# Four quadrants for v's and the inverse's products, new side durations in the planner, two loads on SP's queue, and overwritten products ahead of two transposes, in a two-layer RWKV, pooling and attention trunk

## The chip, the core and the metric

The kernel runs on one core of a Trainium2 chip. A time is the device time of one execution in microseconds; the kernel before is given by the median of three runs. The engines are named as the profile names them: PE (TensorE), ACT (ScalarE), DVE (VectorE), POOL (GpSimd) and SP (SyncE, which only issues DMAs here).

## What is computed

Input x is 1 x 1024 x 1024 in float32. Each of two layers makes one wide projection of x and feeds three branches with it, whose gated sum goes through an output projection and a normalization:

```python
for l in range(DEPTH):
    h = jnp.einsum('bsd,dn->bsn', x, w_in[l]) + b_in[l]
    (u_a, z_a, p_b, z_b, q_c, k_c, v_c, z_c, g_a, g_b, g_c) = _split(h, SPLIT_SIZES)
    o_a = rwkv7_branch(u_a, z_a, ...)
    o_b = pool_branch(p_b, z_b, ...)
    o_c = attention_branch(q_c, k_c, v_c, z_c, cos, sin)
    merged = (sigmoid(g_a) * (o_a @ proj_a[l]) + sigmoid(g_b) * (o_b @ proj_b[l])
              + sigmoid(g_c) * (o_c @ proj_c[l]))
    x = normalize(DEEPNORM_ALPHA * x + merged @ w_out[l]) * ln_g[l] + ln_b[l]
```

The RWKV branch is the long one. For 16 heads of 64, forwards and backwards over 1024 positions, it carries a 64x64 state: `sa = state @ (-kk)`, then `state = state * w + sa b^T + v k^T` and `y = state @ r`. The kernel does it in chunks of 64 positions, which needs the inverse of a triangular matrix in each chunk, and a sequential step over the chunks.

## The kernel before

**Dense products.** Every weight matrix is used in float32 by three products: the weight is split into a high part `wh` (a cast on ACT, L551) and a low part `wl` (a subtraction, L552, on POOL in the RWKV stage and the merge, on POOL or DVE elsewhere), the activations likewise into `xh` and `xl` (or `obh`/`obl`, `och`/`ocl`, `mh`/`ml`). A dense step is three products of 128x512 over one block of 128 rows: L583 (high, high), L584 (low, high) and L585 (high, low). `Dense` makes these steps; a piece of weight is 128x512 values, loaded by SP at L540.

**Stages.** A layer runs `rwkv` (848 dense steps with the recurrence between them), `attention`, `pool`, `proj_bc` (projections of the two branches behind pooling and attention, gated) and `merge` (projection proj_a, the gated sum, then w_out and the normalization, token block by token block). In layer 0 they stand at about 60 to 1222, 1222 to 1600, to 1758, 1758 to 1859 and 1859 to 2065 us; layer 1 follows in the same way.

**What sets the order.** Each engine works through its own queue in order. The order is made when the program is built: pieces of work (`Th`) have a list of steps with an engine and a cost in ns each ("P" PE, "A" ACT, "D" DVE, "G" POOL, "S" SP), needs and gives, and buffers in rings ("m" is a ring of two PSUM buffers of 2 KB per partition). `Sched.run` simulates the engines with these costs and takes what can start soonest, with dense steps as filler. A `side` cost is what a dense step books on other engines (the split of the weight piece). So a changed cost moves instructions on all engines, though it is no instruction itself.

**The recurrence.** For each of 8 pairs of heads (`j`) and 4 quarters (`q`) of the sequence, both directions are prepared together: scores, the inverse by products in f16 (L1054), `nkt` (32 transposes by products with the identity, L1008, two PSUM buffers, two copies) and `av` (16 products of a score block with v, L1022, one PSUM buffer, one copy at L1025); the trace shows each float32 product of this form as two. Then four steps each follow: `A` (products of the state, L1143 and L1146, into the two PSUM tiles `sqp`, `pu` and `py`; then DVE adds u0, L1150), `W` (ACT scales the state, L1154), `B` (four products, L1161, then two ACT copies into `uv`, L1165) and `Cc` (L1175, L1180, then DVE updates the state, L1185). There are 64 `av` and 256 steps in the two layers. `HS[0]` and `HS[1]` are partitions 0 to 63 and 64 to 127: the rows of an operand choose the row half of the array, the partitions of the result the column half, so a 64x64 product takes one quadrant of the array. In `nkt` the products of a group take all four quadrants; in `av` and `B` they take two.

```python
1022  nc.tensor.matmul(ps[HS[h], d, i], lhsT=sc[HS[1 - h], d, c, h, 0:64], rhs=uv[HS[1 - h], n, h, :], ...)
1161  nc.tensor.matmul(pu[HS[h], 128 + 64 * s:192 + 64 * s], lhsT=J["sc", Q][HS[h], d, c, 0, 0:64], rhs=J["u0"][HS[h], d, :], ...)
```

The quarter's end is normalized and transposed (`f5`, L1246, four transposes from `ysq`, which POOL writes at L1241). At the start of each pair, `psk` (L781) and `psr` (L823, from `nx`, which ACT writes at L796) make norms and the rotated copies.

**The other places.** In `attention`, `t1` makes the scores (L1447) from `rawq` and `rawk`, to which DVE applies the rotary embedding (`rope`, L1387 to L1394). In `proj_bc`, ACT writes the high and POOL the low part of `oz`, the result of the RWKV branch, from 32 loads `ozt` (L1772 issues, L1776 casts, L1778 subtracts); the products of `obh` and `och` are gated by DVE (`m`, L1741; `t`, L1752) and added by POOL (L1754). `y` at L1692 is DVE's last product on the pooling branch. In `merge`, `wor` (L1819) loads 16 blocks of w_out, the products of a token block follow (L1842 to L1844), DVE reads the gate `g` at L1810, and `back` (L1883) transposes the normalized block `s`, which POOL finishes at L1873, for the next layer.

Of the kernel before, what the change touches and what calls it, by code (L numbers as in the profile page):

```python
# [10 lines left out]
F32 = mybir.dt.float32  # L11
# [371 lines left out]
def trunk(ctx: ExitStack, tc: tile.TileContext, a: dict, out, dbg=None):  # L383
# [124 lines left out]
    class Dense:  # L508
# [56 lines left out]
        def make(self, src, nk, rhs, evac, halves=(0, 1), needs=(), gives=(), ev=(("A", 570.0),), key=None, ering=(), first=False):  # L565
# [31 lines left out]
            for x in range(len(ids) * len(halves)):  # L597
                for pi, h in [(x % len(ids), halves[x // len(ids)]) if first else (x // len(halves), halves[x % len(halves)])]:
                    for kk in range(min(KP, nk - KP * pi)):
                        last = KP * pi + kk == nk - 1  # L600
                        out_.append(Th(mm(pi, kk, h), [("P", 640.0)],
                                       side=(("A", 307.0), ("G" if self.lo is nc.gpsimd else "D", 620.0 if self.lo is nc.gpsimd else 335.0)) if kk == 0 and h == halves[0] else (),
# [25 lines left out]
    def rwkv(l):  # L628
        P = pc["P"]
        w_in = a["w_in"][l]  # L630
        with ExitStack() as es:
# [136 lines left out]
            def pair_kk(j):  # L768
# [76 lines left out]
                o.append(Th(f5, [("G", 3770.0)]))  # L845
# [151 lines left out]
            def joint(j, q):  # L997
# [16 lines left out]
                def av():  # L1014

                    sc, ps = J["sc", Q], psm.tile([128, 2, 4, 64], F32, tag="m", name="psav")
                    uv = J["uv", j, int(q in (1, 2))]
                    for d in range(2):
                        for i in range(4):
                            c, n, _ = place(d, q, i)  # L1020
                            for h in range(2):
                                nc.tensor.matmul(ps[HS[h], d, i], lhsT=sc[HS[1 - h], d, c, h, 0:64], rhs=uv[HS[1 - h], n, h, :],  # L1022
                                                 start=True, stop=True, skip_group_check=True)
                    yield
                    nc.scalar.copy(sc[:, :, :, 1, 0:64], ps)  # L1025
                return ([Th(nkt, [("P", 930.0), ("A", 500.0), ("A", 500.0)], needs=[("sc", d, Q) for d in range(2)], ring=("m", "m"), gives=[("nkt", Q)])],
                        [Th(av, [("P", 930.0), ("A", 500.0)], needs=[("nt", Q), ("uv" if q in (1, 2) else "uv0", j)], ring=("m",), gives=[("av", Q)])])
# [95 lines left out]
            def seq(j, q):  # L1123
# [4 lines left out]
                def step(i):  # L1128
# [6 lines left out]
                    def A():  # L1135
# [4 lines left out]
                        for d in range(2):  # L1140
                            ar, (c, n, s) = J["ar", d, Q % NB], pl[d]
                            for h in range(2):
                                nc.tensor.matmul(pu[HS[h], 64 * d:64 * d + 64], lhsT=ar[HS[h], c, 0, :], rhs=sbd[d][HS[h]],  # L1143
                                                 start=d == 0, stop=True, skip_group_check=True)
                            for h in range(2):
                                nc.tensor.matmul(py[HS[1 - h], y0 + 64 * s:y0 + 64 * s + 64], lhsT=ar[HS[h], c, 1, :], rhs=sbd[d][HS[h]],  # L1146
                                                 start=d == 0, stop=False, skip_group_check=True)
# [8 lines left out]
                    def B():  # L1156
                        pu, uv = J["p"][1], J["uv", j, io]
                        for d in range(2):
                            c, n, s = pl[d]
                            for h in range(2):  # L1160
                                nc.tensor.matmul(pu[HS[h], 128 + 64 * s:192 + 64 * s], lhsT=J["sc", Q][HS[h], d, c, 0, 0:64], rhs=J["u0"][HS[h], d, :],  # L1161
                                                 start=False, stop=True, skip_group_check=True)
# [804 lines left out]
```

## Time and profile before

| | |
|---|---|
| median of 3 runs | 4117.68 us (4116.34 to 4122.85) |
| profiled execution | 4110.03 us, its span 4107.9 us |
| mean granted PE clock over the span | 0.990 |
| PE busy | 3933.5 us, 96% |
| ACT, DVE, POOL busy | 2224.0, 2344.7, 1653.9 us |
| DMA | 326.41 MB, mean 79 GB/s |

The busy share is a mean over stages with different limits. A row of the timeline gives start and length of an instruction or of a group of like ones; a bracket behind it, as [2.95 <-DVE rawk L1394], says how long the engine had been idle and what ended that. In the table by stretches PEclk is the granted clock as a share of full speed: 0.5 is a stretch wholly at 1.2 GHz, 1.00 one at 2.4. Durations and sums below come from the profiled execution.

### The profile page before, as it was taken

What the parts mean: (1) busy time and instruction counts of PE and PEld (TensorE: products, weight loads), DVE (VectorE), ACT (ScalarE), POOL (GpSimd) and SP (SyncE); (2) the same over time, 40 slices, a digit from 0 to 9 for tenths busy, and PEclk for the clock granted to TensorE, in tenths of its full rate; (3) what the DMA queues carried; (4) which work ended last, traced back from release to release, by engine and by line L of the source; (5) the groups of instructions that cost most, each with busy time, mean ns of one, the idle gap of its engine ahead of it and who ended that gap; (6) DMA issues with size and microseconds to landing.
All of it is one profiled execution on the core that took longest, in us unless ns stands there. A gap on an engine that the chain in (4) does not pass through costs nothing. (4 is left out here: it accounts for less than half of the span.)

```text
span 4107.9 us, 120670 instructions
## 1 busy us (share of the span) xinstructions
PE 3933.5 (96%) x51576; PEld 3060.1 (74%) x51576; DVE 2344.7 (57%) x4233; ACT 2224.0 (54%) x4390; POOL 1653.9 (40%) x2498
## 2 busy tenths in 40 slices
PE   8999999999999999999989999999999999999998
PEld 6677777777777788877767777777777777888777
DVE  3776766665533554545647667766665245454456
ACT  5677787777643442322146777777677434433210
POOL 4343444344433343453233444454434334334532
PEclk9999999999999999999999999999999999999999
DMA  2111111111114442155311111111111244421653
GB/s 90 32 48 43 44 42 45 45 42 44 58 58 119 130 134 91 54 181 192 123 51 30 48 40 44 42 48 40 43 47 54 76 114 133 127 83 55 191 182 116
DMA packets 329192, 326.41 MB, mean 79 GB/s; under 512 B 23536, under 2 KB 264384, under 8 KB 328655
## 3 DMA queue, kind: packets, MB, share of 16 engines
q1 hardware_dynamic: 301551, 233.66, 19.1%
q0 software_dynamic: 27104, 85.04, 5.9%
q8 instruction: 404, 6.62, 0.7%
q14 instruction: 133, 1.09, 0.1%
HBM read 224.86 MB, written 81.99 MB: 75 GB/s over the span
## 5 line engine op out<-in xcount | busy, mean ns | idle before, releaser
L583 PE MATMUL psdn<-xh,wh 128*128 128x512 f32 x3136 | 1331.1, 424 | 9.1 <-ACT wh L551 8.2
L585 PE MATMUL psdn<-xh,wl 128*128 128x512 f32 x3136 | 1240.8, 396 | 9.5 <-POOL wl L552 9.3
L584 PE MATMUL psdn<-xl,wh 128*128 128x512 f32 x3136 | 1236.5, 394 | 0.0
L552 POOL TENSOR_TENSOR wl<-wr,wh 128x512 fp32r<-128x512 f32 (+1 forms) x436 | 599.4, 1375 | 1313.1 <-ACT wh L551 1287.5
L583 PEld LDWEIGHTS psdn<-xh,wh 128*128 128x128 f32 x3136 | 594.5, 190 | 169.0 <-issue 31.0
L585 PEld LDWEIGHTS psdn<-xh,wl 128*128 128x128 f32 x3136 | 593.8, 189 | 151.4 <-POOL wl L552 19.5
L584 PEld LDWEIGHTS psdn<-xl,wh 128*128 128x128 f32 x3136 | 596.2, 190 | 101.0 <-issue 4.8
L551 ACT CAST wh<-wr 128x512 fp32r<-128x512 f32 (+2 forms) x484 | 290.3, 600 | 697.6 <-PE psdn L584 351.1
L1059 ACT CAST U<-pst 64x512 f16<-64x512 f32 x768 | 444.8, 579 | 116.9 <-PE pst L1054 100.1
L1087 DVE TENSOR_TENSOR X<-pst,c 128x512 f16<-128x512 f32 x320 | 219.4, 685 | 198.2 <-PE pst L1054 198.1
L1185 DVE SCALAR_TENSOR_TENSOR sbd<-sqp,wc,sbd 128x64 f32<-128x64 f32 x480 | 113.8, 278 | 216.9 <-PE sqp L1180 156.4
L1165 ACT COPY uv<-sqp 64x128 f32<-64x128 f32 x512 | 131.5, 257 | 85.0 <-PE sqp L1161 76.9
L1054 PEld LDWEIGHTS <-X 64*64 64x64 f16 x6144 | 144.1, 108 | 26.6 <-DVE sc L983 8.4
L1154 ACT ACTIVATE sbd<-sbd,wc 128x64 f32<-128x64 f32 x480 | 140.3, 340 | 43.1 <-PE sqp L1146 30.6
L1071 POOL TENSOR_TENSOR nl<-sc,nh 64x512 f16<-64x512 f32 x128 | 154.7, 1209 | 8.2 <-ACT nh L1068 3.0
L1054 PE MATMUL pst<-U,X 64*64 64x64 f16 x5120 | 153.6, 197 | 2.1 <-ACT U L1059 0.9
L1161 PEld LDWEIGHTS sqp<-u,sc 64*64 64x64 f32 x2048 | 80.1, 133 | 91.4 <-issue 50.2
L978 PE MATMUL pssc<-ar,nk 64*64 64x128 f32 x4096 | 146.4, 274 | 0.4
L1054 PEld LDWEIGHTS <-U 64*64 64x64 f16 x5120 | 113.1, 109 | 44.9 <-issue 14.5
L1054 PE MATMUL pst<-X,U 64*64 64x64 f16 x5120 | 140.3, 194 | 0.3
L1143 PEld LDWEIGHTS sqp<-sbd,ar 64*64 64x64 f32 x2048 | 83.6, 133 | 73.9 <-issue 43.7
L1150 DVE TENSOR_TENSOR u<-sqp,sc 128x128 f32<-128x128 f32 x256 | 73.4, 287 | 113.5 <-PE sqp L1146 61.0
(707 smaller groups left out, 7707.5 us busy)
## 6 DMA issues: line engine op xcount, KB each, us to landing
wr<-in_w_in_dram SPq DMA_DIRECT2D x360, 256.0 KB, 2.9
sga<-gt POOLq DMA_DIRECT2D x96, 256.0 KB, 2.3
g<-sga SPq DMA_DIRECT2D x96, 256.0 KB, 4.4
wr<-in_proj_a_dram SPq DMA_DIRECT2D x64, 256.0 KB, 3.0
sza<-sz POOLq DMA_DIRECT2D x32, 256.0 KB, 3.2
bva<-bv POOLq DMA_DIRECT2D x32, 256.0 KB, 2.5
oa<-o POOLq DMA_DIRECT2D x32, 256.0 KB, 3.0
oat<-oa SPq DMA_DIRECT2D x32, 256.0 KB, 3.6
```

The source lines that it names most:

```text
L551: nc.scalar.copy(hi[:, 0:n, :], r[:, 0:n, :])
L552: self.lo.tensor_tensor(out=lo[:, 0:n, :], in0=r[:, 0:n, :], in1=hi[:, 0:n, :], op=ALU.subtract)
L583: nc.tensor.matmul(ps, lhsT=hi[:, kk, :], rhs=ah, start=(k == 0), stop=False)
L584: nc.tensor.matmul(ps, lhsT=hi[:, kk, :], rhs=al, start=False, stop=False)
L585: nc.tensor.matmul(ps, lhsT=lo[:, kk, :], rhs=ah, start=False, stop=(k == nk - 1))
L978: nc.tensor.matmul(ps[h][HS[h if x == 0 else 1 - h], c, :], lhsT=nk[HS[h], c, x, :], rhs=ar[HS[h], c].rearrange("p a t -> p (a t)"), start ...
L1054: nc.tensor.matmul(ps[HS[1 - h if mir else h], d, c], lhsT=l, rhs=r, start=start and d == 0 and c == 0, stop=stop, skip_group_check=True)
L1059: nc.scalar.copy(dst[HS[h]], ps[HS[1 - h]])
L1071: nc.gpsimd.tensor_tensor(out=nl[HS[h]], in0=sc[HS[h], :, :, h, 0:64], in1=nh[HS[h]], op=ALU.subtract)
L1087: tt(out=x, in0=ps[0], in1=mask(i + 1), op=ALU.mult)
L1154: act(sbd[d], sbd[d], AF.Copy, scale=J["wc", d, Q % NB][:, pl[d][0]:pl[d][0] + 1])
L1165: nc.scalar.copy(uv[HS[h], two, h, :], pu[HS[h], 128:256].rearrange("p (s e) -> p s e", s=2))
```

## The change

1. `av`: products of the two directions alternate, into one PSUM buffer each, and those of direction 1 write the other half of the partitions, so the group takes four quadrants; one copy of 128x512 becomes one of 128x256 and two of 64x256.
2. `B`: the products go by row half to the one or the other `sqp` tile and by direction to the upper or lower partitions, four quadrants; two copies of 64x128 become four of 64x64. In `A`, the products for `py` come ahead of those for `pu`.
3. The planner's costs: the split of a weight piece goes from 307 to 520 ns on ACT, from 620 to 1235 on POOL and from 335 to 602 on DVE, and many others are raised (rope's three DVE steps from 1160 each to 1900, 2070 and 1500).
4. The loads of `ozt` (32) and `wor` (16) are issued by SP in place of POOL.
5. Ahead of the last `f5` of each layer's RWKV stage stand 12 products of 128x512 into the buffer that the transposes then overwrite, and ahead of the first `back` of the last token block of layer 0 stand 20.

Lines move: L1161 is L1164 after, L1165 L1169, L1022 L1023, L1025 L1026 and L1029, L1246 L1252 (its 12 products L1250), L1447 L1453, L1692 L1698, L1772 L1778, L1776 L1782, L1883 L1891 (its 20 products L1889).

```diff
@@ Dense: side cost of a piece
-   side=(("A", 307.0), ("G" if ... else "D", 620.0 if ... else 335.0)) ...
+   side=(("A", 520.0), ("G" if ... else "D", 1235.0 if ... else 602.0)) ...
@@ av
-   sc, ps = J["sc", Q], psm.tile([128, 2, 4, 64], F32, tag="m", name="psav")
+   ps = [psm.tile([128, 4, 64], F32, tag="m", name="psav") for _ in range(2)]
-   for d in range(2):
-       for i in range(4):
+   for i in range(4):
+       for d in range(2):
            for h in range(2):
-               nc.tensor.matmul(ps[HS[h], d, i], lhsT=sc[HS[1 - h], d, c, h, 0:64], ...)
+               nc.tensor.matmul(ps[d][HS[h if d == 0 else 1 - h], i], lhsT=sc[HS[1 - h], d, c, h, 0:64], ...)
-   nc.scalar.copy(sc[:, :, :, 1, 0:64], ps)
+   nc.scalar.copy(sc[:, 0, :, 1, 0:64], ps[0])
+   yield "first"
+   for h in range(2):
+       nc.scalar.copy(sc[HS[h], 1, :, 1, 0:64], ps[1][HS[1 - h]])
@@ step B
-   pu, uv = J["p"][1], J["uv", j, io]
+   p, uv = J["p"][::-1], J["uv", j, io]
-   nc.tensor.matmul(pu[HS[h], 128 + 64 * s:192 + 64 * s], ...)
+   nc.tensor.matmul(p[h][HS[d], 384:448], ...)
-   nc.scalar.copy(uv[HS[h], two, h, :], pu[HS[h], 128:256].rearrange("p (s e) -> p s e", s=2))
+   for d in range(2):
+       nc.scalar.copy(uv[HS[h], pl[d][1], h, :], p[h][HS[d], 384:448])
@@ f5
+   for _ in range(12 if j == NJ - 1 and o == 0 else 0):
+       nc.tensor.matmul(ps.rearrange("p a b -> p (a b)"), lhsT=xh[:, 0, 0:128], rhs=xh[:, 0, 0:512], start=True, stop=True)
@@ rope
-   Th(f1, [("D", 1160.0)]), Th(f2, [("D", 1160.0)]), Th(f3, [("D", 1160.0)], ...)
+   Th(f1, [("D", 1900.0)]), Th(f2, [("D", 2070.0)]), Th(f3, [("D", 1500.0)], ...)
@@ proj_bc, loads of oz
-   nc.gpsimd.dma_start(out=t, in_=oz[k * 128:(k + 1) * 128, hs])
+   nc.sync.dma_start(out=t, in_=oz[k * 128:(k + 1) * 128, hs])
-   load.append(Th(fn, [("G", 1040.0)], lag=LDW, ...))
+   load.append(Th(fn, [("S", 100.0)], lag=LDW, ...))
@@ merge, loads of w_out
-   nc.gpsimd.dma_start(out=t, in_=a["w_out"][l][k * 128:(k + 1) * 128, :])
+   nc.sync.dma_start(out=t, in_=a["w_out"][l][k * 128:(k + 1) * 128, :])
@@ back
+   for _ in range(20 if t == 7 and g == 0 else 0):
+       nc.tensor.matmul(ps.rearrange("p a b -> p (a b)"), lhsT=mh[:, 0, 0:128], rhs=wh[:, 0, 0:512], start=True, stop=True)
```

PE, one step of the recurrence in layer 0: `A`'s products, dense steps, then `B`'s, of before and after (`pu` is `sqp_1641` before and `sqp_1660` after, `py` is `sqp_1640` and `sqp_1659`).

```order
L1143 MATMUL sqp_1641<-sbd0_294,ar_889 64x64 x2
L1146 MATMUL sqp_1640<-sbd0_294,ar_889 64x64 x2
L1143 MATMUL sqp_1641<-sbd1_295,ar_895 64x64 x2
L1146 MATMUL sqp_1640<-sbd1_295,ar_895 64x64 x2
L781 MATMUL psk_1650<-cst_80,sq_1575 128x128 x4
L583 MATMUL psdn_1661<-xh_88,wh_1278 128x512
L584 MATMUL psdn_1661<-xl_89,wh_1278 128x512
L585 MATMUL psdn_1661<-xh_88,wl_1279 128x512
L583 MATMUL psdn_1661<-xh_88,wh_1278 128x512
L584 MATMUL psdn_1661<-xl_89,wh_1278 128x512
L585 MATMUL psdn_1661<-xh_88,wl_1279 128x512
L1161 MATMUL sqp_1641<-u0_1655,sc_949 64x64 x4
```

```order
L1150 MATMUL sqp_1660<-sbd1_295,ar_895 64x64 x2
L583 MATMUL psdn_1634<-xh_88,wh_1236 128x512
L584 MATMUL psdn_1634<-xl_89,wh_1236 128x512
L585 MATMUL psdn_1634<-xh_88,wl_1237 128x512
L583 MATMUL psdn_1634<-xh_88,wh_1236 128x512
L584 MATMUL psdn_1634<-xl_89,wh_1236 128x512
L585 MATMUL psdn_1634<-xh_88,wl_1237 128x512
L1164 MATMUL sqp_1660<-u0_1672,sc_949 64x64
L1164 MATMUL sqp_1659<-u0_1672,sc_949 64x64
L1164 MATMUL sqp_1660<-u0_1672,sc_949 64x64
L1164 MATMUL sqp_1659<-u0_1672,sc_949 64x64
```

`B`'s four products, all into one PSUM tile before, alternate between the two tiles; two dense steps stand ahead of them in both.

PE, the first score products of the attention stage in layer 0 (`pssc`), with the dense products ahead of them (a new number at `psdn` begins a new dense tile), of before and after.

```order
L583 MATMUL psdn_23443<-xh_88,wh_23419 128x512
L584 MATMUL psdn_23443<-xl_89,wh_23419 128x512
L585 MATMUL psdn_23443<-xh_88,wl_23420 128x512
L1447 MATMUL pssc_23485<-rawk_23407,rawq_23327 128x128
L1447 MATMUL pssc_23486<-rawk_23407,rawq_23327 128x128
```

```order
L585 MATMUL psdn_23807<-xh_88,wl_23784 128x512
L583 MATMUL psdn_23855<-xh_88,wh_23820 128x512
L584 MATMUL psdn_23855<-xl_89,wh_23820 128x512
L585 MATMUL psdn_23855<-xh_88,wl_23821 128x512
L583 MATMUL psdn_23855<-xh_88,wh_23820 128x512
L584 MATMUL psdn_23855<-xl_89,wh_23820 128x512
L585 MATMUL psdn_23855<-xh_88,wl_23821 128x512
L1453 MATMUL pssc_23869<-rawk_23770,rawq_23691 128x128
L1453 MATMUL pssc_23870<-rawk_23770,rawq_23691 128x128
```

Before, two steps of the second half's last piece (`psdn_23443`) were still to come behind these products; now that tile is done and two steps of the next are ahead of them: four dense steps later. The first score products of the second, third and fifth tile also move back four steps, those of the fourth and sixth one step.

ACT, the beginning of `proj_bc` in layer 0, of before and after (`y` are the last evacuations of the pooling branch, `wh` the casts of proj_b's and proj_c's pieces, 128x512 and 128x256).

```order
L1689 ACTIVATE y<-psdn,pc 128x512 x2
L551 CAST wh<-wr 128x512
L551 CAST wh<-wr 128x256 x2
L1776 CAST xh<-ozt 128x512 x2
L551 CAST wh<-wr 128x512
L1776 CAST xh<-ozt 128x512
```

```order
L1695 ACTIVATE y<-psdn,pc 128x512 x2
L1782 CAST xh<-ozt 128x512
L551 CAST wh<-wr 128x512
L1782 CAST xh<-ozt 128x512 x2
L551 CAST wh<-wr 128x256
L1782 CAST xh<-ozt 128x512 x3
```

The cast of the first 128x512 piece now stands behind the first cast from `ozt`, which waits for a load that SP issues. On PE, the last `psy` transposes of the RWKV stage stand ten dense steps later than before, and in `merge` SP issues the `wor` loads singly between those of the weights and of the gates.

## Rows read from the trace of the kernel before

**Rows 1.** The page, part 1: busy us, share of the span, instructions.
```profile
PE 3933.5 (96%) x51576; PEld 3060.1 (74%) x51576; DVE 2344.7 (57%) x4233; ACT 2224.0 (54%) x4390; POOL 1653.9 (40%) x2498
```

**Rows 2.** Windows, first RWKV stage: stretch, us, busy by engine, PEclk, DMA share, GB/s.
```profile
130.00:1210.00 1080.00, 1055.24 (x21368) 792.97 (x21365) 691.06 (x1439) 794.59 (x1649) 449.94 (x849) 1.00 0.14 44
200.00:300.00 100.00, 99.39 (x1968) 75.24 (x1964) 73.37 (x142) 80.93 (x165) 49.80 (x99) 1.00 0.14 44
```

**Rows 3.** Timeline, PE: start us, length us, line, operation, count of products.
```profile
427.62 1.16 PE L1008 MATMUL psnt<-cst,nk 64*64 64x64 f32 x64
...
603.35 0.45 PE L1161 MATMUL sqp<-u,sc 64*64 64x64 f32 x8
...
664.45 1.15 PE L1022 MATMUL psav<-uv,sc 64*64 64x64 f32 x32
```

**Rows 4.** Groups by line and form, ACT: busy us, mean ns | idle before.
```profile
L1165 ACT COPY uv<-sqp 64x128 f32<-64x128 f32 x512 | 131.5, 257 | 85.0 <-PE sqp L1161 76.9
...
L758 ACT COPY uv<-psv 64x256 f32<-64x256 f32 x128 | 46.9, 366 | 9.7 <-PE psv L753 7.8
...
L1025 ACT COPY sc<-psav 128x512 f32<-128x512 f32 x64 | 37.4, 584 | 32.2 <-PE psav L1022 16.3 <-POOL nl L1071 8.6 <-PE sqp L1146 4.7
```

**Rows 5.** Timeline, PE, attention of layer 0: [idle before <- what ended it].
```profile
1263.61 2.02 PE L1447 MATMUL pssc<-rawk,rawq 64*128 64x128 f32 x16 [2.95 <-DVE rawk L1394]
...
1406.39 1.46 PE L1447 MATMUL pssc<-rawk,rawq 64*128 64x256 f32 x8 [2.69 <-DVE rawk L1394]
...
1458.23 1.14 PE L1447 MATMUL pssc<-rawk,rawq 64*128 64x256 f32 x8 [0.77 <-DVE rawk L1394]
```

**Rows 6.** Timeline, PE, layer 0: RWKV stage's ends, merge's end.
```profile
67.61 0.66 PE L781 MATMUL psk<-cst,sq 128*128 128x128 f32 x4 [1.28 <-ACT lw L915]
...
80.24 1.12 PE L823 MATMUL psr<-cst,nx 128*128 128x128 f32 x4 [5.89 <-ACT nx L796]
...
1214.83 0.39 PE L583 MATMUL psdn<-xh,wh 128*128 128x512 f32 x1
1215.06 0.39 PE L584 MATMUL psdn<-xl,wh 128*128 128x512 f32 x1
...
1219.79 1.11 PE L1246 MATMUL psy<-cst,ysq 128*128 128x128 f32 x4 [4.11 <-POOL ysq L1241]
...
2062.91 1.97 PE L1883 MATMUL psx<-cst,s 128*128 128x128 f32 x8 [6.31 <-POOL s L1873]
```

**Rows 7.** Windows behind four holes; the granted clock is third from the end.
```profile
1219.00:1223.00 4.00, 3.21 (x10) 2.75 (x11) 0.00 (x0) 0.78 (x1) 1.44 (x3) 0.57 0.07 20
1263.00:1267.00 4.00, 3.39 (x19) 2.89 (x20) 1.90 (x4) 0.00 (x0) 0.00 (x0) 0.59 0.02 4
79.00:86.00 7.00, 5.76 (x16) 4.71 (x17) 0.75 (x1) 1.23 (x2) 1.02 (x3) 0.52 0.10 37
2059.00:2066.00 7.00, 3.10 (x12) 2.85 (x13) 5.38 (x9) 1.68 (x3) 2.81 (x6) 0.51 0.25 82
```

**Rows 8.** Timeline, all engines, the projection behind the pooling stage of layer 0.
```profile
1759.22 0.61 ACT L551 CAST wh<-wr 128x512 fp32r<-128x512 f32 x1
...
1761.07 0.69 DVE L1692 TENSOR_TENSOR y<-y,sz 128x512 f32<-128x512 f32 x1
...
1763.10 0.47 PE L583 MATMUL psdn<-obh,wh 128*128 128x512 f32 x1 [1.87 <-DVE m L1741]
...
1799.04 7.08 DVE L552 TENSOR_TENSOR wl<-wr,wh 128x256 fp32r<-128x256 f32 x1 [0.91 <-ACT wh L551]
...
1802.13 3.70 POOL L1778 TENSOR_TENSOR xl<-ozt,xh 128x512 fp32r<-128x512 f32 x3
...
1806.77 0.79 PE L583 MATMUL psdn<-obh,wh 128*128 128x512 f32 x1 [5.17 <-DVE m L1741]
```

**Rows 9.** Waits: us in total, times, longest us.
```profile
DVE g L1810 <- DMA g<-sga: 49.4, 21, 5.7
```

**Rows 10.** Source view of L1772, the load of ozt from oz.
```profile
DMA to landing us min/median/max: 3.1/5.1/7.2
```

More of the change, by code (lines that the diff above doesn't have):

```diff
@@ L1142, in A @@
                             for h in range(2):
+                                nc.tensor.matmul(py[HS[1 - h], y0 + 64 * s:y0 + 64 * s + 64], lhsT=ar[HS[h], c, 1, :], rhs=sbd[d][HS[h]],
+                                                 start=d == 0, stop=False, skip_group_check=True)
+                            for h in range(2):
                                 nc.tensor.matmul(pu[HS[h], 64 * d:64 * d + 64], lhsT=ar[HS[h], c, 0, :], rhs=sbd[d][HS[h]],
                                                  start=d == 0, stop=True, skip_group_check=True)
[L1145 to L1147 removed]
                         yield
@@ L1556, in attention @@
                     nd = prev if nm != "v" else ([("vt", order[n - 1])] if n >= 1 else [])
-                    dense += dn.tile(w_in[:, col * 128:(col + 1) * 128], 8, xr, qkv_evac(nm, ct, col, dil), needs=nd, gives=[("raw", nm, ct)], key=(col, l))
+                    dense += dn.tile(w_in[:, col * 128:(col + 1) * 128], 8, xr, qkv_evac(nm, ct, col, dil), ev=(("A", 1020.0),), needs=nd, gives=[("raw", nm, ct)], key=(col, l))
                 ro += rope(ct, dil)
@@ L1564, in attention @@
                 col = ZC // 128 + i
-                dense += dn.tile(w_in[:, col * 128:(col + 1) * 128], 8, xr, szc_evac(i), gives=[("szc", i)], ev=(("A", 1140.0), ("D", 600.0)))
+                dense += dn.tile(w_in[:, col * 128:(col + 1) * 128], 8, xr, szc_evac(i), gives=[("szc", i)], ev=(("A", 1366.0), ("D", 700.0)))
             for i in range(24 - NGA, 24):
@@ L1763, in proj_bc @@
                 cs = slice(d * 128, (d + 1) * 128)
-                dense += dn.tile(a["proj_c"][l][:, cs], 2, rh(och, ocl), ev_c(d), ev=(("D", 600.0),), key=("c", l) if d == 0 else None)
-                dense += dn.tile(a["proj_b"][l][:, cs], 6, rh(obh, obl), ev_b(d), ev=(("D", 600.0), ("G", 1225.0)), key=("b", l) if d == 0 else None)
+                dense += dn.tile(a["proj_c"][l][:, cs], 2, rh(och, ocl), ev_c(d), ev=(("D", 686.0),), key=("c", l) if d == 0 else None)
+                dense += dn.tile(a["proj_b"][l][:, cs], 6, rh(obh, obl), ev_b(d), ev=(("D", 686.0), ("G", 1419.0)), key=("b", l) if d == 0 else None)
             load, split = [], []
@@ L1893, in token @@
                     for k in range(8):
-                        d.append(Th(mm(k, n), [("P", 640.0)] + ([("D", 1200.0)] if k == 7 else []), rows=1.0, chain=False,
+                        d.append(Th(mm(k, n), [("P", 640.0)] + ([("D", 1380.0)] if k == 7 else []), rows=1.0, chain=False,
                                     ring=("d",) if k == 0 else (), hold=hold if k < 7 else None, drop=hold if k == 7 else None,
@@ L1897, in token @@
                 o.append(Th(stat, [("D", 200.0), ("A", 100.0), ("D", 300.0)], needs=[("tok", t)]))
-                o.append(Th(norm, [("D", 1270.0), [("G", 1225.0), ("D", 1200.0)], ("S", 100.0)]))
+                o.append(Th(norm, [("D", 1985.0), [("G", 1627.0), ("D", 2344.0)], ("S", 100.0)]))
                 if not last:
-                    o += [Th(back(g), [("P", 428.0), ("A", 480.0), ("D", 602.0)], ring=("m",)) for g in range(2)]
+                    o += [Th(back(g), [("P", 428.0), ("A", 588.0), ("D", 684.0)], ring=("m",)) for g in range(2)]
                 return d, o
@@ L1905, in merge @@
                 for d in range(8):
-                    dense += dn.tile(a["proj_a"][l][:, d * 128:(d + 1) * 128], 8, xr, ev_a(d), halves=(h,), ev=(("D", 2200.0),),
+                    dense += dn.tile(a["proj_a"][l][:, d * 128:(d + 1) * 128], 8, xr, ev_a(d), halves=(h,), ev=(("D", 2950.0),),
                                      key=("a", d, l) if h == 0 else None, gives=[("pa", 8 * h + d)])
```

40 lines of the change are left out of this document (20 added, 20 removed).

## The prediction, made before the changed kernel ran

> **What bounds the kernel now.** The page's first line shows TensorE (PE) busy for 3933.5 of 4107.9 us, against 2224.0 for ScalarE (ACT) [rows 1]. So time is won in two ways only: by shortening what PE does, or by filling its holes. The table by stretches says which way is open where. In the inner part of the first layer's RWKV stage PE works 1055.24 of 1080 us, so its holes there are 24.8 us, while ACT is at 794.59 of 1080, 74%; in the stretch where ACT is fullest (80.93 of 100) PE still works 99.39 [rows 2]. This stage is bound by PE's own instructions. Outside it the holes count: at the ends of the RWKV stage, in the attention stage and in the projection that follows the pooling stage. The reader is to see three things in the rows: how long a group of small products takes in two and in four quadrants of the array [rows 3], which waits make the holes [rows 5, 6, 8], and that PE's granted clock falls to its lower level (1.2 in place of 2.4 GHz) behind some of them [rows 7].
>
> **The quadrants.** 64 products of 64x64 in four quadrants (`nkt`) take 1.16 us; 32 products of the same form in two quadrants (`av`) take 1.15 [rows 3]. Taking off the 0.22 us of the last product's own run, the starts lie 0.94/63 = 15 ns apart in four quadrants and 0.93/31 = 30 ns in two. The eight products of step `B` span 0.45 - 0.22 = 0.23 us, again 30 ns apart or a little more [rows 3]. With four quadrants I take 0.45 us off each of the 64 `av`, 29 us, and 0.115 off each of the 256 `B`, 29 us: **-58 us**. Bounds: 0 if something other than the quadrant holds the products apart, -62 at exactly half.
>
> **What the quadrants cost on ACT.** A copy of 64x128 takes 257 ns, of 64x256 366, of 128x512 584 [rows 4]. So 64 columns cost about 54 ns beside a fixed part, and a 64x64 copy is estimated at 203. `B` gets four of these for two of 257: +298 ns, 76 us over 256 steps. `av` gets three of about 366 for one of 584: +514 ns, 33 us over 64. ACT is given 109 us, 55 in each layer's RWKV stage: from 74% to about 79% busy on the inner stretch's scale, and from 81% to 86% where it is fullest. Nothing of PE's is queued behind that for long while ACT has gaps, since the fullest stretch shows PE waiting only 0.6 us in 100 [rows 2]; what waits for these copies is the next product step, one step later by 0.3 us, with dense products as filler between. Below it is nothing, above it is all 109 us (a rival). I take 12 us, near the end that the fullest stretch shows: **+12**. In `A` the order of the eight products is changed, but the add waits for all of them before and after: nothing.
>
> **Attention.** The first score products of a tile wait for DVE's rope: 2.95 us, later 2.69, and 0.77 in the last tiles [rows 5]; of the long kind there are four in each layer, of the short two. Dearer DVE costs in the planner now put four more dense steps ahead of the first, second, third and fifth of six of these products, one step ahead of the other two. A dense step is three products 0.23 us apart [rows 6], 0.70 us, so four steps are 2.8 us of work in a hole of at most 2.95. Filled: three whole holes, 0.7 of the fourth, and the two short ones, near 10 us per layer. Behind the first hole the clock fell: 0.59 over 4 us [rows 7], so for 0.82 of these 4 us it was at the lower level, 3.3 us in which 1.6 us of work is lost. Three such dips stand behind filled holes in the two layers. Sum 20 + 5 = 25, of which I take **-24**. Bounds: 0, if rope comes later by as much, and -30.
>
> **Ends of the RWKV stage.** At its start, PE waits 5.89 us for ACT's `nx` [rows 6], in layer 1 the same, and the clock is at its lower level for nearly all of the following 7 us (0.52, [rows 7]). The planner moves these transposes eight and four dense steps back in layer 0 and four to eight in layer 1; a part is given back because what they wait for starts later. I take 4 us of each hole, and in each layer the 1.28 of a smaller one ahead of `psk` [rows 6], which two more dense steps cover: **-11** (bounds -2 and -18, the latter with both dips gone). At its end, PE waits 4.11 us for POOL's `ysq` [rows 6]. Ten dense steps, 7 us, are moved ahead of these transposes, which closes the hole; then the 12 overwritten products add 12 x 0.23 = 2.8 us, and the dip behind (0.57 over 4 us, [rows 7]: 1.7 us of lost work) is gone: -4.1 - 1.7 + 2.8 = -3 per layer, **-6**. In the merge of layer 0 the 20 overwritten products, 4.6 us, lie inside the 6.31 us in which PE waits for POOL's `s` [rows 6]. They cost nothing while this wait stands, and 4.6 us if it were gone. What they can give back is the low clock behind it (0.51 over 7 us, [rows 7]) so far as PE works in it: **-1.5**.
>
> **The oz loads on SP.** Before the change, POOL issues them after its own work; a load lands 3.1 us after issue at the least and 5.1 in the median [rows 10]. SP can issue the first as soon as the last `y` product of DVE is done (1761.07 + 0.69 = 1761.8). But ACT's new order sets the cast of the first `ozt` ahead of the cast of the first proj_b piece, which before the change ran at 1759.22, so that its products started at 1763.10 [rows 8]. Now it is load, cast, cast, low part: 1761.8 + 3.1 to 5.1 + 0.6 + 0.6 + 0.7 = 1766.8 to 1768.8, a wait of 4 to 6 us more, and a clock dip with it, 1.7. Against this stands the worst hole of the stage: a 128x256 subtraction on DVE, where a 128x512 product takes 0.69, takes 7.08 us at 1799.04 while POOL works without a break until 1805.83, and PE waits 5.17 [rows 8]. The Trainium skill, page "SBUF — State Buffer", section "Who interferes with whom", states that DVE and GpSimd hold a port pair in turn, whoever starts first; the row agrees, with 7.08 us. Without the DMA issues POOL's runs may break up, or only get shorter. Per layer from +8 to -7; I take +2, **+4** in all. Bounds -14 and +16.
>
> **The w_out loads on SP.** They stand between the weights and gates that the merge waits for; DVE waits 49.4 us for these gates now, 21 times [rows 9]. One load of 512 KB ahead of a gate's 256 KB may delay it by about its own landing time. **+4**, bounds -6 and +20.
>
> **Sum.** -58 + 12 - 24 - 11 - 6 - 1.5 + 4 + 4 = -80.5 us. The profiled execution took 4110.03, 7.65 below the median of the three runs, 4117.68; against the median the forecast is 4037. About 0.2% (8 us) is what a measurement of this kernel can tell from no change.
>
> **The rivals.** (1) *Slower: ACT becomes the bound of the RWKV stage.* If all 109 us of added copies end up as PE waiting (the sum without its +12), the change is -92.5 + 109 = +16.5, 4134 us. It decides from 93% of the copies (101 of 109) on to be told as slower. For it: the copies lie on the sequential chain of 128 steps per layer. Against: PE at 99.39 beside ACT at 80.93 [rows 2]. The Trainium skill, "TensorEngine Tiling (Array Packing)", section "PSUM Bottleneck", warns of this very thing: tiling speeds TensorE up, not the copy out of PSUM. Chance 0.05. (2) *Half of the quadrants' gain comes back as waits* for the longer chain of `u`, copy, next step: +29 on the sum, 4066. For it: each step's chain grows by about 0.3 us of copies and wins 0.115. Chance 0.17. (3) *SP's queue:* the first oz load and the w_out loads both cost their upper bound, +16 and +20 for +4 and +4: 4065. For it: ACT's order in proj_bc. Chance 0.13. (4) *The change does not do what it says:* products in four quadrants wait for each other over PSUM banks or on the common weights path, so nothing is won: +58 and most of the +12 back, 4090. Against: `nkt`, 64 products in 1.16 us [rows 3]. Chance 0.05. The forecast has 0.60.
>
> **The numbers.** The forecast's own range comes from its bounds: 4005 (everything at its good end but one or two) to 4060. With rivals 2 and 3, and some of them together, it reaches to 4085; rivals 1 and 4 lie outside. Faster by over 0.2%: forecast, 2, 3, 4, less a little for mishaps together: 0.92. Slower: rival 1, 0.05. Within: 0.03.
>
> **What would show it.** Right: groups of 32 `av` products near 0.7 us and of 8 `B` products near 0.33 in the timeline; ACT at about 79% and PE still above 97% in the inner RWKV stretch, which is shorter by 25 to 29 us; no 2.7 us hole ahead of the first score products; no low clock behind the last psy transposes. Wrong: `B` groups at 0.45 (rival 4); many new PE waits on `uv` copies (rivals 1, 2); a hole of 6 us or more at the first proj_b products with `xh` from `ozt` as its cause (rival 3). The prediction fails as a whole if the RWKV stage does not get shorter.

## The result and the profile after

The changed kernel takes 4064.52 us (median of 4 runs, 4059.0 to 4072.4) against 4117.01 before: ratio 0.9872, 95% interval 0.9851 to 0.9893. That is 52 us less where 80.5 were forecast. The profiled execution has a span of 4057.2 us, 50.7 less than before.

The page's first part of the kernel after, as [rows 1]:

```profile
PE 3877.1 (96%) x51620; PEld 3004.1 (74%) x51620; DVE 2327.2 (57%) x4233; ACT 2337.1 (58%) x5030; POOL 1647.4 (41%) x2450
```

PE is busy 56 us less and ACT 113 us more, where the prediction's sums for the quadrants were 58 and 109. Part of the 56 has other causes: against the changed kernel without quadrants (run below) PE is busy 46.6 us less and ACT 107.9 us more. So most of what the quadrants were to save on PE is there; the question is what became of it. The span, cut at PE instructions that both kernels have, both layers added (us; the idle time is that in which no product runs; layer 1 begins where layer 0 ends):

```
stretch                                        before   after   change   PE idle before, after
first dense product to first score product     2485.6  2466.6   -19.0    89.6 116.6
from there to proj_bc                            991.4   958.4   -33.0    21.7   1.6
proj_bc                                          202.2   197.8    -4.4    16.8  14.0
merge                                            408.6   412.7    +4.1    37.0  37.7
ahead of the first dense product                  19.9    21.7    +1.8     9.3  10.1
```

The attention stage, proj_bc and the merge together gave what was forecast or more. The RWKV stage was to give 63 us and gave 19 (25, counting that eight dense steps, 5.6 us, have moved into it from attention).

The products themselves, timeline of PE after, as [rows 3]:

```profile
187.26 0.34 PE L1164 MATMUL sqp<-u,sc 64*64 64x64 f32 x8
...
423.85 1.11 PE L1008 MATMUL psnt<-cst,nk 64*64 64x64 f32 x64
...
497.56 0.70 PE L1023 MATMUL psav<-uv,sc 64*64 64x64 f32 x32
```

Eight products of `B` take 0.34 us in place of 0.45, 32 of `av` 0.70 in place of 1.15. The four quadrants work as reckoned. The copies, groups by line and form, as [rows 4]:

```profile
L1169 ACT COPY uv<-sqp 64x64 f32<-64x64 f32 x1024 | 210.8, 206 | 71.0 <-PE sqp L1164 59.6
...
L1029 ACT COPY sc<-psav 64x256 f32<-64x256 f32 x128 | 47.0, 367 | 2.1
...
L1026 ACT COPY sc<-psav 128x256 f32<-128x256 f32 x64 | 23.6, 368 | 16.3 <-POOL nl L1075 9.5 <-PE psav L1023 3.7 <-PE psdn L585 2.2
```

A 64x64 copy takes 206 ns (203 estimated), the three of `av` 367 and 368. The inner RWKV stretch after, as [rows 2]:

```profile
130.00:1210.00 1080.00, 1030.07 (x21308) 766.25 (x21306) 688.58 (x1432) 845.70 (x1961) 455.85 (x850) 1.00 0.14 45
```

ACT goes from 794.59 to 845.70 of 1080 us, 78%; PE falls from 1055.24 to 1030.07. It was this that the prediction did not expect: PE idles 25 us more in this stretch and works 95.4% of it, where the prediction had it above 97%. The waits of PE in the first RWKV stage, after (us in total, times, longest us), and then the three largest of before:

```profile
PE sqp L1164 <- DVE u L1154: 8.5, 16, 1.4
PE sqp L1179 <- ACT uv L1169: 7.2, 16, 0.7
PE sqp L1147 <- DVE y L1196: 6.3, 11, 1.0
PE sqp L1147 <- DVE y L1194: 5.1, 11, 0.9
```

```profile
PE sqp L1161 <- DVE u L1150: 7.1, 15, 1.7
PE psr L823 <- ACT nx L796: 6.1, 2, 5.9
PE sqp L1143 <- DVE sbd L1185: 3.3, 7, 0.8
```

Waits for `uv` and for `y` are new: of the first kind there were 0.8 us before, of the second none.

The ends of the stages, timeline of PE after, as [rows 5, 6]: `psr`, the last `psy` with its 12 overwritten products, the first score products, and `psx` of the merge.

```profile
80.84 0.66 PE L823 MATMUL psr<-cst,nx 128*128 128x128 f32 x4 [1.03 <-ACT nx L796]
...
1215.38 2.88 PE L1250 MATMUL psy<-xh 128*128 128x512 f32 x12
1219.89 0.65 PE L1252 MATMUL psy<-cst,ysq 128*128 128x128 f32 x4 [1.63 <-POOL ysq L1245]
...
1256.58 1.16 PE L1453 MATMUL pssc<-rawk,rawq 64*128 64x128 f32 x16 [1.99 <-DVE rawk L1400]
...
2042.45 1.27 PE L1891 MATMUL psx<-cst,s 128*128 128x128 f32 x8 [1.77 <-POOL s L1879]
```

The holes of 5.89, 2.95 and 6.31 us are 1.03, 1.99 and 1.77. The one at the last `psy` is still there: 1.63 us behind 2.7 us of overwritten products. The clock (third from the end of a row of the windows), as [rows 7], and in proj_bc:

```profile
79.00:86.00 7.00, 5.97 (x31) 4.71 (x30) 1.49 (x2) 3.04 (x5) 2.15 (x7) 1.00 0.14 40
1217.00:1224.00 7.00, 5.37 (x26) 4.21 (x25) 0.00 (x0) 1.28 (x2) 3.35 (x6) 1.00 0.52 177
1740.00:1751.00 11.00, 5.61 (x14) 4.44 (x15) 3.84 (x4) 4.24 (x8) 8.29 (x7) 0.53 0.83 267
```

Behind the start and the end of the RWKV stage it stays at 2.4 GHz, where the rows of before had 0.52 and 0.57. In proj_bc of layer 0 it is at its lower level (1.2 GHz) for most of 11 us. What stands ahead of that, as [rows 8] (ACT, PE, SP's issues, and DVE's last `y`):

```profile
1742.14 0.62 ACT L1782 CAST xh<-ozt 128x512 fp32r<-128x512 f32 x1 [5.51 <-DMA ozt<-oz]
1742.66 0.61 ACT L551 CAST wh<-wr 128x512 fp32r<-128x512 f32 x1
...
1745.39 0.77 PE L583 MATMUL psdn<-obh,wh 128*128 128x512 f32 x1 [6.85 <-DVE m L1747]
...
1739.09 2.71 SPq L1778 DMA_DIRECT2D ozt<-oz  x6
...
1737.46 1.60 DVE L1698 TENSOR_TENSOR y<-y,sz 128x512 f32<-128x512 f32 x1
```

SP issues the first `ozt` load at 1739.09 us, when DVE's last `y` has ended (1739.06). ACT waits 5.51 us for it, casts it, and only then casts the piece of proj_b; the products of that piece wait 6.85 us, 7.06 in layer 1.

### The profile page after: what moved, and what is told of

Read it like the earlier page. It is cut to its first block, busy times and chain, and to the rows that moved or that the text cites. A ratio compares the mean times of both kernels' runs of the same rounds, so it can differ in the third digit from the quotient of the medians.

```text
span 4057.2 us, 121335 instructions
## 1 busy us (share of the span) xinstructions
PE 3877.1 (96%) x51620; PEld 3004.1 (74%) x51620; DVE 2327.2 (57%) x4233; ACT 2337.1 (58%) x5030; POOL 1647.4 (41%) x2450
## 5 line engine op out<-in xcount | busy, mean ns | idle before, releaser
L1169 ACT COPY uv<-sqp 64x64 f32<-64x64 f32 x1024 | 210.8, 206 | 71.0 <-PE sqp L1164 59.6
L624 POOL DMA_DIRECT2D sga<-gt x96 | 54.1, 563 | 238.3 <-ACT gt L623 175.4
L1058 PE MATMUL pst<-U,X 64*64 64x64 f16 x5120 | 143.7, 195 | 4.0 <-ACT U L1063 2.2
L964 POOL TENSOR_TENSOR nk<-ta,k 128x256 f32<-128x256 f32 x128 | 104.5, 820 | 88.1 <-ACT ta L957 85.6
```

The costliest lines, as they stand in the source:

```text
L1058: nc.tensor.matmul(ps[HS[1 - h if mir else h], d, c], lhsT=l, rhs=r, start=start and d == 0 and c == 0, stop=stop, skip_group_check=True)
L1169: nc.scalar.copy(uv[HS[h], pl[d][1], h, :], p[h][HS[d], 384:448])
```

## The experiments

Where two edited kernels are compared, the ratios to the kernel before are given, since that was run anew beside each group. For the RWKV stage a table is used that is worked out from the traces: the time from each product's start on PE to the next one's, put down to the kind of the later, from the first dense product to the first score product of attention, both layers added. It holds work and waits alike. The time just ahead of those score products, 0.8 to 7.4 us, is left out of it. Each column is one execution, and kernels that are alike in this stage differ in it by a few us: the changed kernel and the one with the oz loads planned later (below) by 3.3, `av` alone and both together by 1.9.

```
             before  quadrants  no quadrants  av alone  av alone,     after
                     alone      (rest as      (rest as  after's order
                                changed)      changed)  of queues
av             66.1     35.9        66.8         40.4        41.9       42.2
B             143.2    137.6       136.4        139.8       141.8      119.3
A             144.5    153.7       146.2        139.8       152.4      152.6
Cc            191.9    208.7       195.6        195.0       186.1      201.3
inverse       286.4    308.8       291.6        293.7       293.5      299.0
scores        120.6    130.2       120.3        128.3       128.8      131.1
nkt            73.3     76.3        70.0         72.8        79.3       79.1
dense        1261.7   1269.0      1260.2       1263.3      1256.5     1256.0
all          2478.7   2509.1      2473.0       2454.3      2461.2     2463.6
```

(The rows of smaller kinds are left out. The first two columns have eight dense steps less in the stage, 5.6 us, since these stand behind it there; 24 overwritten products, 5.4 us, stand in the last four columns.)

**The quadrants alone.** Parts 1 and 2 of the change on the kernel before, with the planner's costs for `av` and `B` themselves, nothing else.

> The kernel before with the four quadrants of av and B, the order of A and their costs in the planner alone (parts 1 and 2); the planner's other costs, the loads and the overwritten products stay as before. Theory (part of the gain comes back as waits on ACT's copies and behind A's new order): 25 to 35 us faster than before, 4082 to 4092 us, PE idle in the RWKV stage up by 10 us or more in each layer. Rival (the quadrants pay in full, and the other parts of the change lose in the RWKV stage): 46 to 58 us faster, 4059 to 4071.

Measured: 4146.03 us, ratio 1.0080 (1.0061 to 1.0099): 33 us slower than before. Neither expectation held. `av` falls by 30 us, `B` by 6 only, and everything around them rises. Waits of PE in the first RWKV stage:

```profile
PE sqp L1164 <- DVE u L1154: 15.6, 19, 3.1
PE sqp L1179 <- ACT uv L1169: 10.6, 16, 1.8
PE sqp L1147 <- DVE y L1196: 9.2, 10, 2.2
```

The waits that appeared in the changed kernel are here larger: steps that wait for u, for the copies of `uv` and for y. They are not all of the loss: in the table the inverse alone takes 22 us more.

**The planner's costs alone.** Part 3 on the kernel before.

> The kernel before with the planner's raised costs alone (part 3). Theory: the holes ahead of the first score products are filled and the start of the RWKV stage is better, 25 to 35 us faster than before, 4082 to 4092 us. Rival (the new order loses in the RWKV stage what it wins in attention): within 12 us of before, 4105 to 4117.

Measured: 4072.72 us, 0.9895 (0.9879 to 0.9912): 41 us faster, more than expected. It is most of what the whole change gives. In the traces, 35.7 us apart, the stretch from the first score product to proj_bc gives 30, the one ahead of it 10, proj_bc 14; the merge loses 18. In proj_bc no load is moved here, yet the hole of 5.17 us of [rows 8] is gone; the holes of layer 0 that are left there (PE):

```profile
1743.31 0.47 PE L583 MATMUL psdn<-obh,wh 128*128 128x512 f32 x1 [1.87 <-DVE m L1741]
...
1769.14 0.50 PE L583 MATMUL psdn<-obh,wh 128*128 128x512 f32 x1 [0.38 <-DVE m L1741]
...
1787.37 0.48 PE L583 MATMUL psdn<-och,wh 128*128 128x512 f32 x1 [1.15 <-DVE t L1752]
```

DVE's longest subtraction there takes 2.97 us, where it took 7.08.

**The loads back on POOL.** The changed kernel with part 4 undone.

```diff
-   nc.sync.dma_start(out=t, in_=oz[...])      # Th(fn, [("S", 100.0)])
+   nc.gpsimd.dma_start(out=t, in_=oz[...])    # Th(fn, [("G", 1040.0)]), wor likewise
```

> The changed kernel with the loads of ozt and wor back on POOL and at their old costs (part 4 undone). Theory (SP's queue costs: holes of 6.9 and 7.1 us at the first proj_b products, 5.6 us in each merge, with low clock behind them): 8 to 18 us faster than the changed kernel, 4046 to 4057 us, though the 5.2 us hole behind DVE's long subtraction is back. Rival (SP's queue costs nothing net, since it removes that hole): 4060 to 4070.

Measured: 4061.0 us, 0.9867 (0.9852 to 0.9881): not to be told from the changed kernel. The trace shows two opposite terms: proj_bc is 6.8 and 3.1 us shorter in the two layers, the merge 4.8 and 5.3 longer. SP is the worse queue for `ozt` as it is planned, and by this run the better one for `wor`. The size of that second term is not sure: in the other executions with these loads on SP the merge takes 207.7 to 210.5 us in layer 0 and 203.2 to 208.0 in layer 1, here 213.6 and 209.2. DVE's subtraction of 7.08 us does not come back with POOL's issues; its longest is 1.50 us in layer 0 and 2.97 in layer 1, 1.34 in both layers after the change. What took away most of it was part 3, not part 4.

**No overwritten products.** The changed kernel with part 5 undone.

> The changed kernel without the 12 and 20 overwritten products (part 5 undone). Theory (they keep the clock up for what they cost, 2.8 us in each layer): within 6 us of the changed kernel, 4059 to 4070 us, low clock back behind the last psy transposes and at the start of layer 1. Rival (they keep the clock for much longer than they last): 10 us slower, 4074 or more.

Measured: 4068.85 us, 0.9890 (0.9875 to 0.9904): not to be told from the changed kernel. The last `psy` of layer 0 (PE) and the clock around it:

```profile
1221.12 1.11 PE L1252 MATMUL psy<-cst,ysq 128*128 128x128 f32 x4 [4.34 <-POOL ysq L1245]
...
1218.00:1224.00 6.00, 2.88 (x9) 2.50 (x10) 0.00 (x0) 1.29 (x2) 3.43 (x6) 0.56 0.53 170
```

The hole is 4.34 us, as long as before the change (4.11). So the ten dense steps that were moved ahead do not close it: PE is through them at 1216.8 us, about when it was through ten fewer before (1215.7), and `ysq` comes no earlier (1221.1 us against 1219.8). The products of after fill 2.7 us of such a hole, and the clock is at 1.00 there in place of 0.56.

**No quadrants.** The changed kernel with parts 1 and 2 undone.

> The changed kernel with av, A and B as before (parts 1 and 2 undone), the rest as changed. Theory (in the RWKV stage the four quadrants give PE work back, but ACT's copies and the longer chain of a step take nearly all of it): 4063 to 4076 us, PE idle in the RWKV stage back at about 40 us per layer. Rival (under the new costs the quadrants pay at least half of their 58 us): 4088 us or more.

Measured: 4071.9 us, 0.9895 (0.9878 to 0.9911), as the theory had it. In the table the RWKV stage takes 2473.0 us, with the quadrants 2463.6: of 42 us that `av` (24.6) and `B` (17.1) win, 9 are left, and 10 by the two ratios, whose intervals overlap. With the quadrants PE is idle for 116.6 us of this stage, without them for 76.7.

**Only av in four quadrants.** The changed kernel with A and B as before (part 2 undone).

> The changed kernel with A and B as before (part 2 undone), av in four quadrants. Theory (av pays, since its 64 groups lie off the step's chain; B's four copies and A's order eat what B wins): 5 to 15 us faster than the changed kernel, 4049 to 4060 us. Rival (B pays, av does not): 8 to 20 us slower, 4072 to 4085.

Measured: 4053.58 us, 0.9848 (0.9833 to 0.9862), and 18 us less than without any quadrants, on the same chip with intervals that don't meet. `av` pays: 18.7 of its 26.4 us arrive in the stage's sum (14.7, if the time ahead of the first score products is counted). The waits for u and `uv` in the first RWKV stage:

```profile
PE sqp L1165 <- DVE u L1154: 6.5, 16, 1.8
PE sqp L1179 <- ACT uv L1169: 1.7, 5, 0.6
```

So part 2 costs about 10 us by the ratios (their intervals just overlap) and 9.3 in the table, though `B`'s products are 20 us cheaper with it.

**Two of B's copies on DVE, by direction.**

```diff
-   nc.scalar.copy(uv[HS[h], pl[d][1], h, :], p[h][HS[d], 384:448])
+   (nc.vector.tensor_copy if d else nc.scalar.copy)(uv[HS[h], pl[d][1], h, :], p[h][HS[d], 384:448])
```

> The changed kernel with two of B's four copies (direction 1) on DVE in place of ACT, all queues in the same order otherwise. Theory of ACT's copies: the wait of the next products for uv goes from 7.2 us per layer to under 3, ACT falls by 2 to 3 points, 6 to 15 us faster than the changed kernel, 4049 to 4059 us. Rival (the chain's waits come from the order of A and the planner's misjudged slots, and DVE, on the same chain, only passes the wait on): 4060 to 4070.

Measured: 4067.65 us, 0.9879 (0.9863 to 0.9895): nothing gained. The inner RWKV stretch shows ACT back at 796 of 1080 us, where it was before the change, and PE as idle as after it:

```profile
130.00:1210.00 1080.00, 1029.17 (x21311) 766.91 (x21309) 741.00 (x1688) 796.19 (x1705) 455.64 (x850) 1.00 0.14 45
```

ACT's load is therefore not what makes PE idle. The copies and those that wait for them, groups by line and form:

```profile
L1169 DVE COPY uv<-sqp 64x64 f32<-64x64 f32 x512 | 116.1, 227 | 238.9 <-ACT uv L1169 227.7
...
L1179 PE MATMUL sqp<-uv,nk 128*64 128x64 f32 x1920 | 108.5, 234 | 21.2 <-DVE uv L1169 20.1
```

DVE's copies stood 227.7 us in wait for ACT's: four copies in a row as before, only on two engines. Both pairs read the same two PSUM tiles; the next run parts them.

**Two of B's copies on DVE, by PSUM tile.** The same edit with `if h` in place of `if d`.

> The changed kernel with B's copies parted by PSUM tile: the two from the one tile on ACT, the two from the other on DVE, so that nothing sets one pair behind the other (where they were parted by direction, DVE's pair waited for ACT's). Theory (what eats B's gain is the length of the step's chain, four copies in a row, and not ACT's load): the next products' wait for uv falls from 7 to 10 us per layer to under 4, 6 to 14 us faster than the changed kernel, 4050 to 4059 us. Rival (it is A's order or the planner's slots): 4060 to 4070, with the waits for y and u as they were.

Measured: 4072.84 us, 0.9888 (0.9871 to 0.9905): again nothing, rather worse. DVE's copies no longer wait for ACT's:

```profile
L1169 DVE COPY uv<-sqp 64x64 f32<-64x64 f32 x512 | 113.9, 222 | 131.7 <-PE sqp L1164 124.5
...
L1179 PE MATMUL sqp<-uv,nk 128*64 128x64 f32 x1920 | 109.0, 234 | 17.8 <-DVE uv L1169 15.7 <-ACT raw L666 0.8 <-ACT sq L774 0.3
```

In the trace the shortest time from `B`'s first product to `Cc`'s goes from 1.31 to 1.04 us (0.81 with the two copies of before), but three quarters of the steps take more than 2.12 us, where it was 1.90 after; DVE's queue, with 222 ns per copy, is on the same chain. The expected 6 to 14 us did not come, so this edit does not show that a shorter chain would pay; it did not make the common step shorter.

**A's order.** The changed kernel with A's pairs in the order pu, py, py, pu.

> The changed kernel with A's products in the order pu, py, py, pu, so that the first pair needs only the state and not the reading of y, and pu's last pair still ends A. Theory (A's new order sets the wait for y at the head of the step): the 11.4 us of waits for y per layer fall by half, 4 to 10 us faster than the changed kernel, 4054 to 4061 us. Rival (the wait for y is passed through either way, since pu's last pair stands behind py): within 3 us, 4061 to 4068.

Measured: 4065.97 us, 0.9878 (0.9861 to 0.9894), the rival's number. The wait for `y` is no longer in the list of PE's waits; at A's head stands the one for the state:

```profile
PE sqp L1152 <- DVE sbd L1191: 2.4, 6, 0.6
```

PE's idle time in the stage falls from 116.6 to 99.4 us. But A's share of the table is 152.3 us, against 152.6, and the time is the same, so the idle time that went did not shorten the step. A's order costs nothing here, as the prediction had it.

**After's order, with A and B as before.** `B`'s cost in the planner stays as changed, so every queue has the changed kernel's order, instruction by instruction, but for the ACT copies; A's and B's products and B's two copies are those of before.

```diff
-   Th(B, [("P", 240.0), ("A", 400.0)])
+   Th(B, [("P", 130.0), ("A", 780.0)])     # on the kernel with av alone
```

> The changed kernel's order of every queue, instruction by instruction (B's cost in the planner as changed), but with A's and B's products and B's two copies as before; av in four quadrants. It differs from the changed kernel by B and A themselves, and from the kernel with av alone by the planner's slots. Theory of the chain (four copies in a row lengthen each step by 0.5 us, and that is what loses): as fast as with av alone, 4048 to 4059 us, PE idle ahead of A and C back to 10 us and less in each. Theory of the slots (the raised cost of B sets the steps where they have to wait, and B's quadrants themselves pay): slower than the changed kernel by what the quadrants won on PE, 4070 to 4085 us, with the idle times as in the changed kernel.

Measured: 4058.32 us, 0.9871 (0.9855 to 0.9888). The time lies at the slow end of the first expectation (4048 to 4059); the ratio is that of the changed kernel, 0.9872. So neither theory holds whole, and the table says how the time is made up. Against after, in the same order: `B` +22.5, `Cc` -15.2, all else -9.7, together -2.4, which is within what two executions differ by. Against av alone: +6.9, with A at +12.6 and `nkt` at +6.5 and `Cc` and dense at -8.9 and -6.8. So in this order B's quadrants win nothing net of what comes with them (two more copies, A's order), and the order that the planner makes of B's raised cost loses about 7, or 9 by the ratios, whose intervals overlap a little. The waits:

```profile
PE sqp L1165 <- DVE u L1154: 8.4, 16, 1.6
PE sqp L1147 <- DVE sbd L1189: 2.6, 5, 0.9
```

Those for `uv` and `y` are gone with the two copies; the one for u, 8.4, has stayed with the order.

**The first oz loads planned later.** On the changed kernel; the loads stay on SP.

```diff
-   needs=[("oas", l, n - 6)] if n > 5 else (), gives=[("oal", l, n)]
+   needs=[("oas", l, n - 6)] if n > 5 else [("y", 5)], gives=[("oal", l, n)]
```

> The changed kernel with the first six oz loads planned after the last y of the pooling stage, still on SP's queue, so that ACT's cast of the first proj_b piece stands ahead of the first ozt cast again. Theory (the new hole is ACT's order, not the queue): the holes of 6.9 and 7.1 us at the first proj_b products fall to about 2 and the low clock behind them goes, proj_bc 4 to 7 us shorter in each layer, 4050 to 4057 us in all. Rival (DVE's long subtraction and its hole of 5.2 us come back in its place): 4060 to 4068.

Measured: 4049.65 us, 0.9841 (0.9824 to 0.9858). ACT's cast of the proj_b piece (first row) stands ahead of the first `ozt` again, its products wait 1.86 us, and in layer 0 the clock stays up (in layer 1 it is 0.84 over 3750 to 3761 us, where after has 0.69 over 3759 to 3770):

```profile
1735.49 0.61 ACT L551 CAST wh<-wr 128x512 fp32r<-128x512 f32 x1
...
1739.37 0.48 PE L583 MATMUL psdn<-obh,wh 128*128 128x512 f32 x1 [1.86 <-DVE m L1747]
...
1740.00:1751.00 11.00, 10.81 (x47) 8.36 (x45) 4.30 (x7) 3.51 (x8) 4.77 (x4) 1.00 0.93 296
```

proj_bc is 5.9 and 4.5 us shorter in the two layers, and no other hole has taken the place of this one. In the changed kernel's plan the first six loads needed nothing (the `()` of the edit), so the planner set them, and with them ACT's first casts, early; on the chip SP issued the first only when the last `y` was through, as the rows of after show.

**Both together.** av alone in four quadrants, and the oz loads planned later.

> av in four quadrants, A and B as before, and the first oz loads planned after the last y (the two edits that were faster than the changed kernel, together; all else as changed). If they lie in different stages they add: 11 + 15 us under the changed kernel, 4036 to 4042 us. If one only moved its wait into the other's stage: 4045 or more.

Measured: 4041.96 us, 0.9817 (0.9802 to 0.9832): faster than both kernels. The two edits lie in different stages and add: by the ratios they take 0.0024 and 0.0031 off the changed kernel's, together 0.0055, which is what is measured.

## Why the prediction was right, and where its sum was off

The direction and the range (4005 to 4085) held; the point, 4037, was 27 us too low. The make-up of the sum did not hold. The quadrants with their cost were to bring 46 of the 80.5 us and brought about 10 (the run without quadrants against the changed kernel); the other terms were to bring 34.5 and brought about 43. Most of the gain is that of the planner's costs, 41 us by themselves. That the time fell on the number of the second rival (4066), half of the quadrants' gain lost as waits, is in part luck: more than half of that gain was lost, and other terms gave more than forecast. Step by step:

- **The quadrants, -58.** The mechanism and the single prices were right: 0.45 and 0.11 us per group, as in the rows above. Counted from start to start, with the waits ahead of their first products, `av` and `B` won 42 us against the kernel without quadrants.
- **Their cost, +12. This step failed.** It was sized by ACT's load ("PE waiting only 0.6 us in 100"), and the load was the wrong measure: with ACT back at its old load PE is idle as long. The cost is +32 (42 won, 9 left). About 8 of it come with `av` (26.4 won, 18.7 arrive). With `B` all of its gain is lost, and more. In one and the same order, `B` with its two copies and A as before is as fast: what `B`'s products win, `Cc` and its neighbours take. And the order made of `B`'s raised cost is about 7 us worse than with the old cost. That it is the two more copies which lengthen the step (0.81 to 1.31 us at the shortest from `B`'s products to the next ones) is the reading of the new waits for `uv`; no run shows it by itself, since the edits that moved copies to DVE did not make the common step shorter. With the other old costs the loss is more than the gain: 33 us slower than before, for which no run parts the causes. The page "TensorEngine Tiling (Array Packing)" of the Trainium skill, "PSUM Bottleneck", states that the copy out of PSUM may become the bottleneck once tiling has made TensorE faster. Here the copying engine was not full, at 78%, and moving half of `B`'s copies off it won nothing.
- **Attention, -24.** Right: 33 us less in that stretch, 27 without the dense steps that left it; the planner's costs alone give 30 there.
- **Start of the RWKV stage, -11.** Right: `psr` and `psk` take 12.5 us less in the start-to-start sums (30.5 to 19.5 and 20.4 to 18.9), and the low clock is gone.
- **Its end, -6.** Half right. Ten dense steps were to close the hole and did not: without the overwritten products it is still 4.34 us. With these the clock stays up, as forecast; the time of the kernel without them cannot be told from that with them.
- **The end of the merge, -1.5.** As described: a rest of 1.77 us, clock up.
- **oz on SP, +4.** The first wait was reckoned at 4 to 6 us more than 1.87 and is 5.0 and 5.2 more; the low clock behind it costs more than the 1.7 us allowed: 0.53 over 11 us in layer 0 and 0.69 over 11 us in layer 1 are up to 5.2 and 3.4 us of work. Against it, DVE's 7.08 us subtraction is gone in both layers; but mostly the costs did that, not the missing issues on POOL. By the run with the loads on POOL, SP costs proj_bc 9.9 us in the two layers. The prediction read DVE's 7.08 us as agreeing with the rule of the Trainium skill, "SBUF — State Buffer", "Who interferes with whom", that whoever issues first gets the shared port pair. The rows show DVE held up beside POOL's run, but not that order: DVE's subtraction starts at 1799.04 us and POOL's run at 1799.07, and spans on POOL are rough:

```profile
1799.07 2.55 POOL L1778 TENSOR_TENSOR xl<-ozt,xh 128x512 fp32r<-128x512 f32 x2
```

- **w_out on SP, +4.** The sign was wrong: the merge is about 5 us longer in each layer with both loads on POOL (5.6 to 11.5 us longer in the two layers together than in the other executions with the loads on SP).

The first rival (ACT the bound) is out by the run with the copies on DVE. The fourth (no overlap of quadrants) is out by the rows. Of the third, SP's queue, the half on `oz` is there, the half on w_out is not. Two numbers beside the sum do not follow from their own terms: the fourth rival's 4090 (4037 + 58, less most or all of the 12, is 4083 to 4089), and the bound of -62 for the quadrants (half of 0.93 and of 0.23 us per group is -59). What stays open is which part of the step takes `B`'s gain, and whether some cost between the old and the new for `B`, or a form of `B` whose results need two copies only, would keep part of its 20 us.

## What to carry to other kernels

Before a group of products on a sequential chain is made shorter, count what then stands between its last product and the next step: a product gain of 0.11 us bought with two more copies in a row of 206 ns was no gain here, though the copying engine was idle for a fifth of the time. The same edit off the chain (`av`) paid 18 us. When a load moves to another queue, look at what the order behind it assumes of its arrival: here the two loads on SP won nothing that can be told as first planned (4064.52 against 4061.0 us on POOL), and planning the start of the first ones later won 13 us by the ratios.

## What was not expected

- The planner's costs alone, which are no instruction, gave 41 us; the quadrants alone, which make PE's products shorter, lost 33.
- Behind one hole of 6.85 us, ahead of the proj_b products, the clock was 0.53 over 11 us; behind the holes of 2.95 and 4.11 us of before it was 0.59 and 0.57 over 4 us [rows 7].
- Two engines that copied from the same two PSUM tiles did not overlap: 227.7 us of waits of DVE for ACT, gone from that row when the copies were parted by tile. Which results the two engines write changed with it, so that the tiles are the reason is argued, not shown.
